# A state space layer between large matrix products: response matrices stored lag by lag and loaded a tile ahead, transposes one piece later, and the small products that prepare them four at one priority

## The chip, the core and the metric

The kernel runs on one core of one Trainium2 chip. The metric is the device time of that core in microseconds (us), from the start of the program to its end, in fp32 throughout. The kernel before took 2952.3, 2959.95 and 2960.65 us in three runs; the median is 2959.95.

## The reference, cut to what matters

A decoder trunk of two layers works on 256 positions of 2048 numbers. Each layer is a token mixer, an attention to 256 rows of memory (4 heads of 512) and an MLP with a hidden width of 8192 and a squared ReLU, each with an RMSNorm ahead of it and its result added to x. The mixer of layer 0 is a gated MLP. The mixer of layer 1 is a state space layer, and the change is there:

```python
lam_bar = jnp.exp(lam * dt)                      # 128 groups x 64 complex states
b_bar = ((lam_bar - 1.0) / lam)[..., None] * bmat
u = (h @ w_in).reshape(bsz, seq, 128, 16)        # 128 groups of 16 channels
bu = einsum('gpc,bsgc->sbgp', b_bar, u)
states = scan over s of (states = lam_bar * states + bu)
y = einsum('gcp,sbgp->bsgc', cmat, states).real + d_skip * u
val, gate = split(gelu(y) @ w_out + b_out, 2)
x = x + val * sigmoid(gate)
```

The scan is not run position by position. The 256 positions are cut into 32 chunks of T = 8. Inside a chunk the output is a product of the chunk's inputs with a matrix of responses to each lag (with d_skip at lag 0); the state that a chunk leaves behind is another product of its inputs; states are carried over chunks; and what the carried state adds to a chunk's outputs is a third product. The three matrices depend on the weights alone.

## The kernel before, in words

**The large products.** Nearly all of the time goes into products of the activations with weights. To keep fp32 accuracy on TensorE (PE), a weight tile of 128 x 1024 numbers (512 KB, `wraw`, four buffers) is loaded by SyncE's queue (line 118), rounded by ScalarE (ACT) into `whi` (L101), and what the rounding leaves is computed by VectorE (DVE) into `wlo` (L102); both have three buffers. The activations are split the same way. A product is then three matmuls: high by high, high by low, low by high (L145 to L147, in the MLP L558 to L560; with the roles exchanged two matmuls of 512 and 256 columns, L163 and L165). One weight tile with its 12 matmuls is called a *piece* here. Each function for large products calls `tick` after every piece (L148, L561).

**What sets the order.** The kernel is written in a framework that puts every operation into one list with priorities, by default in the order in which the program issues it. From this list it makes one queue for each engine and gives out the buffers; each engine then works strictly through its own queue. Work besides the large products comes in by `tick`: `at(delay, fn)` issues `fn` a number of pieces later (L76), and the list `side` gives out one function every `every` pieces (L81 to L88), at a lower priority: `later(100)` puts its operations some 100 places further back among the others, one by one, so that neighbours in the program can end up apart. Every load and store named below, other than of weights, goes by GpSimd's queue (POOL), which issues its DMAs in order, and a DMA into a buffer waits there until the buffer is free.

**The preparation** (`ssm_prep`) runs as side work under the MLP of layer 0. The 128 groups are taken in 32 quads of four, with three side functions for each. `quad` loads the quad's weights `bcq` (L769), turns the sign of half of them on DVE (L770) and computes `bb`. `quad_q` computes `qt`, 16 columns for each of nine powers (0 to 8), stores powers 1 to 8 as Qd (L796), and multiplies `bb` with `qt` in four small matmuls, one for each group, 32 rows of one PSUM bank each (L799). `kd`, 15 lags by 16 numbers on 128 partitions, gets zeros for the seven negative lags by POOL (L802), lags 1 to 7 by ACT, lag 0 with d_skip by DVE, and is stored as Kd (L806). `quad_p` computes the matrix for the states, transposes it on PE (L814) and stores it as Pd (L817). Eight groups, two quads, share one tile of Pd, Qd and Kd in memory (half `l` = q % 2), so there are 16 of each. In Kd the 15 lags of one input channel, half and group stand together: 15 x 16 numbers in a row.

**The state space stage** (`s5`) takes the product with `b_w_in` in four tiles of 512 columns, `n` = 0 to 3, of eight pieces each; a tile's small work runs under the pieces of the next ones. After the tile's product, DVE and ACT copy it to `u` (L853, L856). Then, by `follow`: two pieces later `inputs` transposes u (eight transposes, L867) and ACT copies it to `us` (L868); three pieces later `own` loads four tiles of `pq` from Pd and multiplies us with them (64 small matmuls, L881) into `z`; five pieces later `states` transposes z (L897) into `vv`; from six to nine `carry` runs the scan over chunks on DVE; after 13 and 15 `outputs` loads `dq` from Kd and `qq` from Qd, two of each at a time, and multiplies us with dq (L932) and vv with qq (L938); after 17 `features` applies the gelu (`y`) and transposes back (L950). Each load is written where its product is (`load`, L837 to L840), and the buffers bound how early it can run: four for pq, three for dq, two for qq. dq takes a window of eight lags for each position j in the chunk, in the address pattern `[[16, T], [8 * row, 16], [row, 8], [1, P]]`: 1024 runs of 128 numbers (512 bytes). pq and qq are read in rows of 4 KB. At the end of the stage come the products with `b_w_out`, whose results go by way of `val` and `gat` into x (L998 to L1010).

## Time and profile before

| | |
|---|---|
| three runs, median (us) | 2952.3 to 2960.65, 2959.95 |
| the profiled execution, its own time (us) | 2960.98 |
| its span, first to last instruction (us) | 2959.3 |
| mean clock granted to TensorE | 0.988 |
| PE busy | 2883.9 us, 97% of the span |
| DVE busy | 1834.4 us, 62% |
| ACT busy | 1337.5 us, 45% |
| POOL busy | 169.0 us, 6% |
| moved by DMA | 581.60 MB, mean 197 GB/s |

The profile is of one execution. A row of matmuls names line, tile, shape and how many stand together (x8); PEld is the loading of the stationary operand, which runs beside PE. A matmul in fp32 (the small ones here) is made in two passes and counts as two. A busy time is the sum of the durations, in which matmuls overlap, so that an engine at 100% can still be slower than at full clock; the granted clock (1.00 is full speed) tells that. A wait is put down to what ended it last. In rows of DMAs the time is that from issue to landing.

### The profile page before, as it was taken

What the parts mean: (1) busy time and instruction counts of PE and PEld (TensorE: products, weight loads), DVE (VectorE), ACT (ScalarE), POOL (GpSimd) and SP (SyncE); (2) the same over time, 40 slices, a digit from 0 to 9 for tenths busy, and PEclk for the clock granted to TensorE, in tenths of its full rate; (3) what the DMA queues carried; (4) which work ended last, traced back from release to release, by engine and by line L of the source; (5) the groups of instructions that cost most, each with busy time, mean ns of one, the idle gap of its engine ahead of it and who ended that gap; (6) DMA issues with size and microseconds to landing.
All of it is one profiled execution on the core that took longest, in us unless ns stands there. A gap on an engine that the chain in (4) does not pass through costs nothing.

```text
span 2959.3 us, 39341 instructions
## 1 busy us (share of the span) xinstructions
PE 2883.9 (97%) x15238; PEld 2379.4 (80%) x15238; DVE 1834.4 (62%) x2548; ACT 1337.5 (45%) x1714; POOL 169.0 (6%) x288
## 2 busy tenths in 40 slices
PE   8999999999999999999997899999999999999998
PEld 6878888888878778778875678888888888888886
DVE  5665655585768778677565455755556555465555
ACT  6435544445434434344453344544454434344443
POOL 1000000000011111111012100000000000000000
PEclk9999999999999999999998999999999999999999
DMA  8766666568666667666689957665566666666665
GB/s 278 213 180 191 193 178 179 170 179 239 190 201 213 206 208 218 205 206 203 215 221 236 206 177 211 192 178 180 169 187 189 187 188 188 186 191 187 188 186 150
DMA packets 180460, 581.60 MB, mean 197 GB/s; under 512 B 38592, under 2 KB 38896, under 8 KB 179504
## 3 DMA queue, kind: packets, MB, share of 16 engines
q1 hardware_dynamic: 140864, 509.67, 57.0%
q0 software_dynamic: 39264, 69.35, 9.2%
q8 instruction: 119, 1.95, 0.3%
q14 instruction: 69, 0.57, 0.1%
q10 hardware_dynamic: 144, 0.07, 0.0%
HBM read 553.88 MB, written 24.90 MB: 196 GB/s over the span
## 4 chain that ended last, share of the span: by engine, by line
PE 88%; DMA 6%; issue 3%; DVE 2%; ACT 1%; POOL 0%; SPq 0%; DVEq 0%; ACTq 0%; POOLq 0%
PE acc L163 23%; PE acc L165 12%; PE acc L560 8%; PE acc L558 8%; PE acc L559 8%; PE acc L146 8%; PE acc L147 7%; PE acc L145 7%; DMA dq<-Kd 1%; DMA qq<-Qd 1%; PE ps L799 1%; PE ps L494 1%; PE ps L438 1%; DMA wraw<-in_b_w_in 1%; DVE wlo L102 1%
## 5 line engine op out<-in xcount | busy, mean ns | idle before, releaser
L102 DVE TENSOR_TENSOR wlo<-wraw,whi 128x1024 fp32r<-128x1024 f32 x952 | 1164.4, 1224 | 891.1 <-ACT whi L101 888.7
L101 ACT CAST whi<-wraw 128x1024 fp32r<-128x1024 f32 x952 | 1002.1, 1053 | 1322.2 <-PE acc L163 409.3
L163 PE MATMUL acc<-act,whi 128*128 128x512 f32 x3072 | 1084.1, 396 | 0.6 <-ACT whi L101 0.6
L165 PE MATMUL acc<-act,wlo 128*128 128x256 f32 x3072 | 864.8, 282 | 0.9 <-DVE wlo L102 0.8
L163 PEld LDWEIGHTS acc<-act,whi 128*128 128x128 f32 x3072 | 576.0, 188 | 136.5 <-issue 4.6
L165 PEld LDWEIGHTS acc<-act,wlo 128*128 128x128 f32 x3072 | 580.2, 189 | 6.3 <-issue 3.0
L146 PE MATMUL acc<-wlo,act 128*128 128x512 f32 x1248 | 494.8, 396 | 13.8 <-DVE wlo L102 13.6
L145 PE MATMUL acc<-whi,act 128*128 128x512 f32 x1248 | 496.1, 397 | 9.6 <-ACT whi L101 9.6
L147 PE MATMUL acc<-whi,act 128*128 128x512 f32 x1248 | 492.6, 395 | 0.0
L560 PE MATMUL acc<-whi,hl 128*128 128x512 f32 x992 | 396.4, 400 | 0.0
L558 PE MATMUL acc<-whi,hh 128*128 128x512 f32 x992 | 396.0, 399 | 0.0
L559 PE MATMUL acc<-wlo,hh 128*128 128x512 f32 x992 | 395.0, 398 | 0.0
L146 PEld LDWEIGHTS acc<-wlo,act 128*128 128x128 f32 x1248 | 238.0, 191 | 69.0 <-DVE wlo L102 21.2
L145 PEld LDWEIGHTS acc<-whi,act 128*128 128x128 f32 x1248 | 238.1, 191 | 62.7 <-ACT whi L101 12.3
L147 PEld LDWEIGHTS acc<-whi,act 128*128 128x128 f32 x1248 | 237.9, 191 | 48.9 <-DVE act L102 0.4
L560 PEld LDWEIGHTS acc<-whi,hl 128*128 128x128 f32 x992 | 186.3, 188 | 48.6 <-issue 4.4
L559 PEld LDWEIGHTS acc<-wlo,hh 128*128 128x128 f32 x992 | 186.3, 188 | 48.4 <-issue 3.6
L558 PEld LDWEIGHTS acc<-whi,hh 128*128 128x128 f32 x992 | 186.3, 188 | 46.8 <-issue 3.2
L542 DVE SCALAR_TENSOR_TENSOR x<-acc,r,x 128x512 f32<-128x512 f32 x62 | 43.6, 745 | 11.7 <-PE acc L560 11.7
L176 ACT ACTIVATE junk<-x 128x512 f32<-128x512 f32 x56 | 35.4, 632 | 24.4 <-DVE x L535 13.9
L938 PE MATMUL ps<-qq,vv 64*32 64x128 f32 x512 | 14.9, 350 | 32.3 <-DMA qq<-Qd 32.3
L524 DVE SCALAR_TENSOR_TENSOR r<-r 128x512 f32<-128x512 f32 x64 | 44.2, 690 | 1.4
(288 smaller groups left out, 1721.3 us busy)
## 6 DMA issues: line engine op xcount, KB each, us to landing
wraw<-in_f_w_up SPq DMA_DIRECT2D x256, 512.0 KB, 3.7
wraw<-in_f_w_down SPq DMA_DIRECT2D x256, 512.0 KB, 3.7
wraw<-in_a_w_in SPq DMA_DIRECT2D x64, 512.0 KB, 4.6
wraw<-in_x_w_q SPq DMA_DIRECT2D x64, 512.0 KB, 3.7
wraw<-in_x_w_k SPq DMA_DIRECT2D x64, 512.0 KB, 3.7
wraw<-in_x_w_v SPq DMA_DIRECT2D x64, 512.0 KB, 3.7
wraw<-in_x_w_o SPq DMA_DIRECT2D x64, 512.0 KB, 3.7
wraw<-in_b_w_out SPq DMA_DIRECT2D x64, 512.0 KB, 4.5
```

The costliest lines, as they stand in the source:

```text
L101: self.nc.scalar.copy(out=hi, in_=src)
L102: self.nc.vector.tensor_tensor(out=lo, in0=src, in1=hi.bitcast(F32), op=ALU.subtract)
L145: nc.tensor.matmul(out[t], ah[:, kt, sl], hi[:, kk, :], start=st, stop=False)
L146: nc.tensor.matmul(out[t], ah[:, kt, sl], lo[:, kk, :], start=False, stop=False)
L147: nc.tensor.matmul(out[t], al[:, kt, sl], hi[:, kk, :], start=False, stop=en)
L163: nc.tensor.matmul(acc[:, f, :], hi[:, kk, sl], both[:, kt].rearrange("p a s -> p (a s)"), start=st, stop=False, skip_group_check=True)
L165: nc.tensor.matmul(acc[:, f, 0:S], lo[:, kk, sl], ah[:, kt, :], start=False, stop=en, skip_group_check=True)
L524: nc.vector.scalar_tensor_tensor(out=r, in0=r, scalar=0.0, in1=r, op0=ALU.max, op1=ALU.mult)
L542: nc.vector.scalar_tensor_tensor(out=xc, in0=acc[:, t, :], scalar=r2[:, t:t + 1], in1=xc, op0=ALU.mult, op1=ALU.add)
L558: nc.tensor.matmul(acc[:, t, :], ah[:, kt % 4, sl], hi[:, kk, :], start=st, stop=False)
L559: nc.tensor.matmul(acc[:, t, :], ah[:, kt % 4, sl], lo[:, kk, :], start=False, stop=False)
L560: nc.tensor.matmul(acc[:, t, :], al[:, kt % 4, sl], hi[:, kk, :], start=False, stop=en)
```

## The change

Four things are changed.

- The four products of a quad in `quad_q` get the same priority: the g-th is issued with its priority raised by g, the number of places that it stands behind the first.
- Kd has another layout: the lag comes ahead of half and group, so that for one input channel and one lag the 2 x 4 x 16 numbers of the tile stand together. A quad's `kd` is stored by four DMAs instead of one, one for each group, 16 partitions each with rows of 16 numbers. The window of eight lags that dq reads is then one row of 1024 numbers (4 KB) for each position and channel.
- The loads are taken out of `own` and `outputs`. `fetch` issues them: the four pq of tile 0 ahead of the loop, those of tile n + 1 four pieces after tile n's product, dq and qq of tile n six and eight pieces after it. dq, qq and pq have four buffers each. To make room, `y` takes the buffer of `z`, and `val` and `gat` take the buffers of pq.
- `inputs` and `own` come one piece later (3 and 4 instead of 2 and 3); `states`, `carry`, `outputs` and `features` stay.

```diff
         mk = lambda nm, sh: [self.dram.tile(sh, F32, name=f"{nm}{q}") for q in range(G // 8)]
         self.Pd = mk("Pd", [P, 2, 4, P])
         self.Qd = mk("Qd", [2, 64, 2, 4 * P])
-        self.Kd = mk("Kd", [32, 2, 4, NL, 16])
+        self.Kd = mk("Kd", [16, NL, 2, 4, 16])
         self.TC1 = self.const.tile([P, 3, G // 2], F32, name="TC1")
         self.TC2 = self.const.tile([P, 3, 2, G // 2], F32, name="TC2")
         sg = pool.tile([P, 1], F32, name="sg", bufs=1)
...
             nc.gpsimd.dma_start(out=self.Qd[q // 2][q % 2].rearrange("p r n -> r p n"), in_=qt[:, 1:])
             kp = self.ps([P, T, 16])
             for g in range(4):
-                nc.tensor.matmul(kp[32 * g:32 * g + 32], bb[:, g], qt[:, 0:T, g, :], start=True, stop=True,
-                                 skip_group_check=True)
+                with self.tc.high_priority(offset=g):
+                    nc.tensor.matmul(kp[32 * g:32 * g + 32], bb[:, g], qt[:, 0:T, g, :], start=True, stop=True,
+                                     skip_group_check=True)
             kd = pool.tile([P, NL, 16], F32, name="kd", bufs=2)
             nc.gpsimd.memset(kd[:, 0:T - 1, :], 0.0)
             nc.scalar.copy(out=kd[:, T:, :], in_=kp[:, 1:, :])
             v.scalar_tensor_tensor(out=kd[:, T - 1, :], in0=eye, scalar=dsk[:, q:q + 1], in1=kp[:, 0, :],
                                    op0=ALU.mult, op1=ALU.add)
-            nc.gpsimd.dma_start(out=self.Kd[q // 2][:, q % 2].rearrange("k t l c -> t k (l c)"), in_=kd)
+            for t in range(4):
+                nc.gpsimd.dma_start(out=self.Kd[q // 2][:, :, q % 2, t], in_=kd[32 * t:32 * t + 16])
         def quad_p(q):
             bcq, bb, tq = e.pop(q)
...
             yT = self.new_act()
             st = {}
-            def load(src, nm):
-                t = sp.tile([P, 2, 4, P], F32, name=nm, bufs={"pq": 4, "dq": 3, "qq": 2}[nm])
+            ahead = {}
+            def load(src, nm, shape):
+                t = sp.tile(shape, F32, name=nm, bufs={"pq": 4, "dq": 4, "qq": 4}[nm])
                 nc.gpsimd.dma_start(out=t, in_=src)
                 return t
+            def fetch(nm, n, i):
+                if nm == "pq":
+                    t = load(self.Pd[4 * n + i], nm, [P, 2, 4, P])
+                elif nm == "qq":
+                    t = load(self.Qd[4 * n + i].rearrange("l p r n -> (l p) r n"), nm, [P, 2, 4 * P])
+                else:
+                    kd = self.Kd[4 * n + i]
+                    t = load(bass.AP(tensor=kd.tensor, offset=kd.offset,
+                                     ap=[[P, T], [(2 * T - 1) * P, 16], [1, T * P]]), nm, [P, T * P])
+                ahead[nm, n, i] = t
             def chunks(n, acc):
...
                 for h in range(2):
                     pz = self.ps([P, 2, 2, 2, 64])
                     for i in range(2):
-                        pq = load(self.Pd[4 * n + 2 * h + i], "pq")
+                        pq = ahead.pop(("pq", n, 2 * h + i))
                         for l in range(2):
                             for t in range(4):
                                 nc.tensor.matmul(pz[32 * t:32 * t + 32, i, l].rearrange("p r s -> p (r s)"),
...
                 if half == 0:
                     st[n] += [[self.ps([P, 4, P]) for _ in range(2)]]
                 py = st[n][2]
-                row = (2 * T - 1) * 16
                 for i in (2 * half, 2 * half + 1):
-                    kd = self.Kd[4 * n + i]
-                    dq = load(bass.AP(tensor=kd.tensor, offset=kd.offset,
-                                      ap=[[16, T], [8 * row, 16], [row, 8], [1, P]]), "dq")
-                    qq = load(self.Qd[4 * n + i].rearrange("l p r n -> (l p) r n"), "qq")
-                    qv = qq.rearrange("p r a b -> p r (a b)").rearrange("p r (j t c) -> p r t j c", t=4, c=16)
+                    dq = ahead.pop(("dq", n, i)).rearrange("p (j l t c) -> p l t j c", j=T, l=2, t=4)
+                    qq = ahead.pop(("qq", n, i))
+                    qv = qq.rearrange("p r (j t c) -> p r t j c", t=4, c=16)
                     for l in range(2):
                         for t in range(4):
-                            nc.tensor.matmul(py[l][32 * t:32 * t + 32, i, :], us[:, 2 * i + l, t, :], dq[:, l, t, :],
+                            nc.tensor.matmul(py[l][32 * t:32 * t + 32, i, :], us[:, 2 * i + l, t, :], dq[:, l, t],
                                              start=(i == 0), stop=False, skip_group_check=True)
                     for r in range(2):
                         for l in range(2):
...
             def features(n):
                 py = st.pop(n)[2]
-                y = sp.tile([P, T, 4, 2, 16], F32, name="y", bufs=1)
+                y = sp.tile([P, T, 4, 2, 16], F32, name="y", tag="z", bufs=1)
                 for l in range(2):
                     nc.scalar.activation(out=y[:, :, :, l, :].rearrange("p j i c -> p i j c"),
                                          in_=py[l].rearrange("p i (j c) -> p i j c", j=T), func=AF.Gelu)
...
             def follow(n):
-                self.at(2, lambda: inputs(n))
-                self.at(3, lambda: own(n))
+                for i in range(4):
+                    if n + 1 < NCH:
+                        self.at(4, lambda i=i: fetch("pq", n + 1, i))
+                    self.at(6 + i // 2 * 2, lambda i=i: fetch("dq", n, i))
+                    self.at(6 + i // 2 * 2, lambda i=i: fetch("qq", n, i))
+                self.at(3, lambda: inputs(n))
+                self.at(4, lambda: own(n))
                 self.at(5, lambda: states(n))
                 self.at(6, lambda: [carry(n, 2, 15), carry(n, 4, 7, 2)])
                 self.at(7, lambda: [carry(n, c, 1, 4) for c in (8, 12, 16)])
...
                 self.at(15, lambda: outputs(n, 1))
                 self.at(17, lambda: features(n))
+            for i in range(4):
+                fetch("pq", 0, i)
             for n in range(NCH):
                 acc = self.gemm_tok(hT, a["b_w_in"], n)
                 if n == 0:
...
                 cs = slice(j * NB, (j + 1) * NB)
                 bv = self.bc(sp, a["b_b_out"][j * NB:(j + 1) * NB])
                 bg = self.bc(sp, a["b_b_out"][D + j * NB:D + (j + 1) * NB])
-                val = sp.tile([P, 2, NB], F32, name="val", bufs=1)
-                gat = sp.tile([P, 2, NB], F32, name="gat", bufs=1)
+                val = sp.tile([P, 2, NB], F32, name="val", tag="pq", bufs=4)
+                gat = sp.tile([P, 2, NB], F32, name="gat", tag="pq", bufs=4)
                 b2 = lambda b: b.unsqueeze(1).broadcast_to([P, 2, NB])
                 if j == 1:
                     for t in range(2):
```

The order of TensorE's queue in the preparation, at the first quad: whi and wlo belong to the MLP's product, `bb` and `qt` to the quad. First the order of before.

```order
L559 MATMUL acc<-wlo,hh 128x512
L799 MATMUL ps<-qt,bb 32x128
L560 MATMUL acc<-whi,hl 128x512
L799 MATMUL ps<-qt,bb 32x128
L558 MATMUL acc<-whi,hh 128x512
L799 MATMUL ps<-qt,bb 32x128
L559 MATMUL acc<-wlo,hh 128x512
L799 MATMUL ps<-qt,bb 32x128
```

Each of the four stands alone there. The same place with the change:

```order
L559 MATMUL acc<-wlo,hh 128x512
L801 MATMUL ps<-qt,bb 32x128 x4
L560 MATMUL acc<-whi,hl 128x512
L558 MATMUL acc<-whi,hh 128x512
L559 MATMUL acc<-wlo,hh 128x512
```

The four products now stand together. Over the whole preparation the 128 products stand in 95 stretches before (81 of one, 2 of two, 5 of three, 7 of four) and in 32 of four now.

POOL's queue in the preparation, from one load of bcq to the next, first before; the numbers behind Qd, Kd and Pd count the tiles in memory.

```order
L769 DMA bcq<-in_b_bc 128x256
L796 DMA Qd_5542<-qt 2x64x512
L806 DMA Kd_5558<-kd 4x32x240
L802 MEMSET kd 128x112
L817 DMA Pd_5526<-po 128x512
```

That is one store for each of the three matrices. The same quad with the change:

```order
L770 DMA bcq<-in_b_bc 128x256
L797 DMA Qd_5542<-qt 2x64x512
L809 DMA Kd_5558<-kd 240x1x16 x4
L820 DMA Pd_5526<-po 128x512
L804 MEMSET kd 128x112
```

One store of Kd became four, and the memset of a later kd stands ahead of the Pd store in some quads and behind it in others.

POOL's queue in the state space stage, from the loads of the last tile's pq (Pd_5536 to 5539) on: Kd_5560 to 5563 and Qd_5544 to 5547 belong to the second tile (n = 1), Kd_5564 to 5567 and Qd_5548 to 5551 to the third.

```order
L839 DMA pq<-Pd_5536 128x1024
...
L839 DMA dq<-Kd_5563 128x8x128
L839 DMA qq<-Qd_5546 128x1024
L839 DMA qq<-Qd_5547 128x1024
L839 DMA dq<-Kd_5564 128x8x128
L839 DMA dq<-Kd_5565 128x8x128
L839 DMA qq<-Qd_5548 128x1024
L892 MEMSET vv 128x2x16
```

The loads of two tiles stand mixed there. With the change, from the same four loads on:

```order
L844 DMA pq<-Pd_5536 128x1024
...
L844 DMA dq<-Kd_5564 128x1x1024
L844 DMA qq<-Qd_5548 128x1024
L844 DMA dq<-Kd_5565 128x1x1024
L844 DMA qq<-Qd_5549 128x1024
L844 DMA dq<-Kd_5566 128x1x1024
L844 DMA qq<-Qd_5550 128x1024
```

Before, loads of the second tile (Kd_5563, Qd_5546 and 5547) still stood behind the last tile's pq; now they stand ahead of it, and dq and qq of the third tile follow it directly, two by two. On TensorE's queue the first transposes of u stand behind as many gemm matmuls as before, counted from the stage's start 135 in the first tile (96 of the first tile's own product and 39 of the next), 82, 25 and 25 in the turns after it; the products with pq stand behind one matmul more in the first two turns and nine more in the last two. The loads of dq and qq of the first tile stand where TensorE has reached the last pieces of the MLP ahead of the stage.

## Prediction

> **What bounds the kernel now.** I read the page's 40 slices first, then the busy time by stretch, then TensorE's waits in the one stretch that stands out, and last the timeline inside it. The first block has PE's row of the slices (tenths of 74 us each). The second has two stretches: us, then busy time and count for PE, PEld, DVE, ACT and POOL, granted clock, DMA share, GB/s.
>
> ```profile
> PE   8999999999999999999997899999999999999998
> ```
> ```profile
> 780.00:1410.00 630.00, 630.00 (x3197) 497.94 (x3197) 476.61 (x749) 263.69 (x321) 93.49 (x160) 1.00 0.69 208
> 1480.00:1720.00 240.00, 199.02 (x1743) 153.77 (x1742) 129.98 (x272) 102.62 (x180) 38.04 (x48) 0.90 0.87 211
> ```
>
> TensorE (PE) is the bound nearly everywhere. While the prep runs under the first layer's MLP (780 to 1410 us) it is busy for all of 630 us; there, time is won only by giving it less to do. In the state space stage (1480 to 1720 us) it stands idle for 240 - 199.0 = 41.0 us, its clock falls to 0.90, and the DMA engines are 0.87 busy. Its waits in that stage (total us, times, longest):
>
> ```profile
> PE ps L938 <- DMA qq<-Qd: 32.3, 8, 9.0
> PE ps L867 <- ACT u L856: 5.0, 4, 2.4
> ```
>
> Most of it is waiting for matrices that are loaded just before use. A wait costs more than its length. The timeline (start, us, what, idle before) around the longest:
>
> ```profile
> 1575.10 1.11 PE L938 MATMUL ps<-qq,vv 64*32 64x128 f32 x32 [8.97 <-DMA qq<-Qd]
> ...
> 1580.19 0.63 PE L146 MATMUL acc<-wlo,act 128*128 128x512 f32 x1
> 1580.61 0.63 PE L147 MATMUL acc<-whi,act 128*128 128x512 f32 x1
> ```
>
> After 9 us without work the matmuls start 0.42 us apart; at full clock, below, it is 0.228.
>
> **Part 1: prep's products in fours.** Two pieces of PE's timeline: the four products of a quad with gemm matmuls between them (each product is two passes, so x2), and a quad whose four happen to stand together already (x8).
>
> ```profile
> 810.51 0.39 PE L558 MATMUL acc<-whi,hh 128*128 128x512 f32 x1
> 810.74 0.40 PE L559 MATMUL acc<-wlo,hh 128*128 128x512 f32 x1
> 811.07 0.41 PE L799 MATMUL ps<-qt,bb 128*32 128x128 f32 x2
> 811.40 0.50 PE L560 MATMUL acc<-whi,hl 128*128 128x512 f32 x1
> 811.84 0.41 PE L799 MATMUL ps<-qt,bb 128*32 128x128 f32 x2
> ```
> ```profile
> 922.77 0.28 PE L165 MATMUL acc<-act,wlo 128*128 128x256 f32 x1
> 922.88 0.39 PE L163 MATMUL acc<-act,whi 128*128 128x512 f32 x1
> 923.11 0.28 PE L165 MATMUL acc<-act,wlo 128*128 128x256 f32 x1
> 923.32 0.43 PE L799 MATMUL ps<-qt,bb 128*32 128x128 f32 x8
> 923.68 0.50 PE L163 MATMUL acc<-act,whi 128*128 128x512 f32 x1
> 924.02 0.28 PE L165 MATMUL acc<-act,wlo 128*128 128x256 f32 x1
> ```
>
> One product alone: 811.84 - 811.07 = 0.77 us from one to the next, less the gemm matmul between them (0.23, from 810.51 to 810.74) leaves 0.53. Four together: a pair of L165 and L163 takes 0.34 (922.77 to 923.11); from 923.11 to 924.02 are 0.91 us with one pair, so 0.91 - 0.34 = 0.57. A stretch of products costs about 0.53 to 0.57 whether it has one or four. In the order of before the 128 products stand in 95 stretches, in that of the change in 32. That takes away 63 x 0.53 = 33.4 us, all on PE in a stretch where PE never waits.
>
> What could give it back is the feeder. VectorE has 476.6 us of work in 630, which would be 80% of the shorter 597, and PE shows no wait there; I count nothing. The same quads now send their lag products out in four stores instead of one, each on POOL's queue: three more issues, in runs of 64 bytes (one lag of 16 numbers) instead of 960. Behind them in POOL's queue stand the memset of a later kd, which waits for the stores, the Pd store and the load of the next bcq, and for bcq waits DVE's sign flip (L770), a few instructions on in the queue that also splits the weights. The rows: POOL's wait ahead of the bcq load, the Kd store's issue (min, median, max), and three DMAs with KB each and median us to landing.
>
> ```profile
> POOL bcq L769 <- DVE tq L789: 80.8, 23, 7.6
> ```
> ```profile
> L806 POOL DMA_DIRECT2D Kd<-kd x32: 700/722/734, 814.9 to 1395.8; - x32
> ```
> ```profile
> pq<-Pd POOLq DMA_DIRECT2D x16, 512.0 KB, 7.6
> dq<-Kd POOLq DMA_DIRECT2D x16, 512.0 KB, 18.5
> ...
> Kd<-kd POOLq DMA_DIRECT2D x32, 120.0 KB, 5.5
> ```
>
> In 23 of 32 quads POOL reaches that load 80.8 / 23 = 3.5 us early. Three more issues take 3 x 0.72 = 2.2 of it. How long four stores of short runs take to land, no row shows. Bounds: below, four small stores (16 of 32 partitions each, so 15 KB, half the bytes in all) land sooner than the one of 120 KB (5.5), which gains nothing on PE; above, they grow like the load with the most runs: dq has 1024 runs and takes 18.5, pq has 128 and the same bytes and takes 7.6, a factor of 2.4, so 5.5 x 2.4 = 13.4. I take about the present landing, since in bytes and in POOL's cover they are nearest to that row, and 2 us in all for quads without cover.
>
> The Trainium skill, "DMA: Bandwidth & Descriptors", section "Specifications", speaks against this edit: transfers below 512 bytes miss line rate, because the DMA engine reads, modifies and writes. No run here shows such stores yet; by this rule the upper bound is the nearer one, and the sum is that of the second rival.
>
> **Part 2: the stage at full pace.** What would the stage's work take without waits? The counts come from the groups of the stage, the times from a piece where nothing waits.
>
> ```profile
> L938 PE MATMUL ps<-qq,vv 64*32 64x128 f32 x512 | 14.9, 350 | 32.3 <-DMA qq<-Qd 32.3
> L932 PE MATMUL ps<-dq,us 128*32 128x128 f32 x256 | 12.3, 315 | 0.4 <-ACT vv L901 0.3
> ...
> L881 PE MATMUL ps<-pq,us 128*32 128x128 f32 x256 | 9.3, 307 | 0.3
> ```
> ```profile
> 1595.98 1.95 PE L881 MATMUL ps<-pq,us 128*32 128x128 f32 x64
> ...
> 1598.43 0.40 PE L147 MATMUL acc<-whi,act 128*128 128x512 f32 x1
> ...
> 1602.53 0.39 PE L147 MATMUL acc<-whi,act 128*128 128x512 f32 x1
> 1602.76 1.04 PE L897 MATMUL ps<-ident,z 128*128 128x128 f32 x8
> 1603.73 0.64 PE L932 MATMUL ps<-dq,us 128*32 128x128 f32 x16
> 1604.30 0.69 PE L938 MATMUL ps<-qq,vv 64*32 64x128 f32 x32
> 1604.92 0.64 PE L932 MATMUL ps<-dq,us 128*32 128x128 f32 x16
> ```
>
> From 1598.43 to 1602.53 are 18 gemm matmuls: 0.228 each. Eight transposes take 0.97 (1602.76 to 1603.73), 16 of L932 0.57, 32 of L938 0.62, 64 of L881 1.95. Of the 1743 matmuls 1024 are of these three lines and 104 are transposes; 615 are gemm. Sum: 615 x 0.228 = 140.1, 4 x 1.95 = 7.8, 13 x 0.97 = 12.6, 16 x 0.57 = 9.1, 16 x 0.62 = 9.9: 179.5. The stage takes 240, so 60.5 us are over: 41.0 idle, 19.5 at the slow clock.
>
> What of it goes? The loads are made about a turn ahead. A turn (one tile of 512 columns) is 96 x 0.228 + 1.95 + 3 x 0.97 + 4 x (0.57 + 0.62) = 31.5 us. In the order of the change dq and qq of a tile are issued as the products of the tile before give up their buffers, some 29 us before use, and pq likewise; against landings of 18.5 and 7.6 (qq, in the same queue, lies between) the waits of 32.3 end, with the slow clock behind them. dq also lies in memory in runs of 4 KB now, like pq. The first tile's twelve loads are issued before and at the stage's start, in the last pieces of the MLP.
>
> What stays? The transposes one piece later: as the order has it, the first ones of each tile stand behind as many gemm matmuls as before (39 in the first turn, 25 in the third); only the pq products behind them move, by 1 matmul in two turns and 9 in the others. So I keep 4.3 of the 5.0 us of waiting for u (its copies are paced by the same weight splits), and take the longer room for the copy of us as worth nothing, up to 1 us. 2.2 stay for the change between small products and gemm matmuls (20 times 0.11: the L163 at 923.68 above is followed after 0.34 instead of 0.23), and 2 for the weight loads that share the first microseconds with four matrices. 60.5 - 8.5 = 52.0 go.
>
> The shared buffers (y with z, val and gat with pq) put no wait in: z of a tile is read out a piece after it is written and y comes pieces later, and pq is done long before val. Without that cover a wait would be one piece, 2.7 us, for a tile.
>
> **The sum.** The profiled execution took 2961.0 (span 2959.3 and 1.7 around it): 2961.0 - 33.4 + 2 - 52.0 = 2877.6. It stands 1.0 over the median of 2959.95, so 2877.
>
> **The rivals.** First, the loads are early and still late, since the DMA engines are the bound. A turn moves 12 matrices and 8 weight tiles of 0.524 MB, 10.5 MB. The fastest stretch of the stage:
>
> ```profile
> 1600.00:1605.00 5.00, 5.00 (x73) 3.90 (x76) 2.18 (x2) 3.09 (x5) 0.30 (x1) 1.00 1.01 404
> ```
>
> At 404 GB/s a turn's bytes take 26.0 us of 31.5, at the stage's present 211 they take 49.8. The first is against this rival, the second for it; dq's short runs are the likely reason of the 211, and they go. Half way, 37.9, three turns are late by 6.4 each: 2877 + 19 = 2896, with ends of 2887 and 2877 + 3 x 18.3 = 2932. A mechanism that would bring it: dq uses half of the DMA engines, which then carry 8.4 / 16 + 2.1 / 8 = 0.79 MB a turn each; at 404 / 16 = 25 GB/s that is 31.1 us, no room at all. That is how the skill's page on DMA ("Why a DMA increments its semaphore by 16 and not by 1", on how many engines) reads for a source whose outermost size is 8, with an exception for some copies from GpSimd. No run here shows which holds.
>
> Second, slower: the short stores hold up prep. The place is POOL's memset and the bcq load behind it; the price 13.4 - 5.5 + 2.2 - 3.5 = 6.6 us a quad, on DVE and so on PE, 32 times: 211, so 3088. It decides from the point where the net delay passes (33.4 + 52) / 32 = 2.7 us a quad. Against it: 18.5 was measured with qq in the same queue at a share of 0.87, prep has 0.69 and a quarter of the bytes.
>
> Third, PE's saving in prep comes to nothing because DVE takes over: 2877 + 33 = 2910. For it, 80% busy in bursts; against it, no wait of PE in 630 us.
>
> That the change does not do what it says is not left open: the order shows both moves.
>
> **How the numbers follow.** My forecast (2868 to 2887) has 0.62, the first rival 0.19, the third 0.07, the second at its price 0.07, a part of it that eats up the gain 0.02, anything else on the fast side 0.03. Under 0.3%, 9 us, a measurement of this kernel tells nothing from no change. So faster 0.91, same 0.02, slower 0.07. The range reaches from 2868 to 2918: forecast, third rival and most of the first, about 0.84.
>
> **What would show it.** Right: prep's products only as x8 in the timeline, and some 33 us less from the first quad's to the last's; no wait of PE for qq, dq or pq, and the stage's clock near 1.00. Wrong: a wait of PE for wlo in prep with DVE waiting for bcq (second rival), PE waits for dq or qq in the second half of a turn and weights landing over 10 us (first), or DVE near 100% in prep (third).

## The result, and the profile after

The change takes 2885.2 us (median of four runs, 2881.5 to 2887.5) where the kernel before takes 2956.7 beside it: a ratio of 0.9757, with a 95% interval of 0.9743 to 0.9772. That is 71.5 us less, about 2.4%; 2877 was forecast, with a range of 2868 to 2918. The profiled execution took 2886.2, with a span of 2884.4.

First the slices of PE after, then its busy times (columns as before): the stretch of the preparation, and the stage from its first gemm matmul to the first L163 behind it.

```profile
PE   8999999999999999999989999999999999999998
```
```profile
780.80:1374.00 593.20, 593.20 (x3177) 486.69 (x3177) 473.32 (x747) 260.70 (x320) 141.67 (x256) 1.00 0.72 217
1443.80:1770.00 326.20, 313.10 (x2305) 251.37 (x2304) 204.18 (x343) 162.46 (x253) 30.62 (x57) 0.98 0.82 236
```

The same stage before, as a row of its own:

```profile
1480.20:1845.50 365.30, 324.28 (x2306) 257.29 (x2305) 205.08 (x343) 162.95 (x253) 42.33 (x56) 0.93 0.82 211
```

The stage is 39 us shorter: 41.0 us of idle time have become 13.1, and the clock has risen from 0.93 to 0.98. What PE still waits for in it (us, times, longest):

```profile
PE ps L884 <- ACT u L873: 8.3, 3, 4.0
PE acc L146 <- DVE wlo L102: 2.3, 4, 0.8
PE acc L145 <- ACT act L101: 1.4, 1, 1.4
```

Four waits of 0.6 us and less are left out. The waits for qq (32.3) are gone, and none for dq or pq has come. The waits for u, 5.0 before, have grown. In the preparation the products stand together, as PE's timeline at the first quad shows:

```profile
807.79 0.40 PE L559 MATMUL acc<-wlo,hh 128*128 128x512 f32 x1
808.12 0.43 PE L801 MATMUL ps<-qt,bb 128*32 128x128 f32 x8
808.47 0.50 PE L560 MATMUL acc<-whi,hl 128*128 128x512 f32 x1
808.81 0.39 PE L558 MATMUL acc<-whi,hh 128*128 128x512 f32 x1
```

Since the order of the large products is the same in both kernels, the start of one and the same gemm matmul can be looked up in each timeline. That cuts each run in pieces (us). "Preparation" is from the MLP's product under which it begins (783.7 before) to the state space stage, "stage" the row above; "first part" is the stage's first 192 gemm matmuls; "behind" goes from the stage's end to one of the last gemm matmuls, 37 us before the end of the program.

| kernel | preparation | stage | first part | rest of it | behind |
|---|---|---|---|---|---|
| before | 696.4 | 365.3 | 57.7 | 307.6 | 1076.4 |
| the change | 663.1 | 326.2 | 58.3 | 267.9 | 1077.1 |
| fours alone | 663.7 | 364.7 | 58.9 | 305.8 | 1076.3 |
| Kd lag by lag alone | 696.4 | 349.1 | 54.6 | 294.5 | 1075.9 |
| loads ahead alone | 696.4 | 335.6 | 61.9 | 273.7 | 1076.4 |
| buffers alone | 696.4 | 335.8 | 60.6 | 275.2 | 1077.2 |
| early transposes | 663.1 | 325.6 | 58.0 | 267.6 | 1076.4 |
| small work later | 662.9 | 325.2 | 54.7 | 270.5 | 1076.4 |
| first loads held back | 663.0 | 325.5 | 48.8 | 276.7 | 1076.5 |
| dq by eight DMAs | 663.0 | 329.9 | 48.8 | 281.2 | 1076.6 |
| dq channel first | 665.1 | 329.8 | 54.0 | 275.8 | 1076.8 |
| stores doubled | 664.8 | 326.4 | 59.3 | 267.1 | 1077.1 |
| grouped, later | 663.1 | 329.6 | 52.7 | 276.9 | 1076.8 |
| grouped, near | 663.9 | 337.1 | 58.3 | 278.7 | 1076.8 |

So the two profiles differ by 33.3 us in the preparation, 39.1 in the stage, and 3 in the 780 us ahead of both, where nothing was changed: the profiled execution of before was the slowest of all there (783.7 us to the start of the preparation's MLP, 777.2 to 782.9 in the other runs). The gain in the stage lies wholly behind its first part, which takes 57.7 us before and 58.3 after.

### The profile page after: what moved, and what is told of

The parts are those of the page before. It is cut to its first block, busy times and chain, and to the rows that moved or that the text cites. A ratio compares the mean times of both kernels' runs of the same rounds, so it can differ in the third digit from the quotient of the medians.

```text
span 2884.4 us, 39580 instructions
## 1 busy us (share of the span) xinstructions
PE 2837.0 (98%) x15238; PEld 2365.6 (82%) x15238; DVE 1831.7 (64%) x2548; ACT 1332.5 (46%) x1714; POOL 205.4 (7%) x384
## 4 chain that ended last, share of the span: by engine, by line
PE 90%; DMA 4%; DVE 3%; issue 2%; ACT 1%; POOL 0%; SPq 0%; DVEq 0%; ACTq 0%; POOLq 0%
PE acc L163 24%; PE acc L165 12%; PE acc L560 8%; PE acc L559 8%; PE acc L558 8%; PE acc L146 8%; PE acc L147 8%; PE acc L145 8%; DVE wlo L102 1%; DMA wraw<-in_b_w_in 1%; PE ps L494 1%; PE ps L438 1%; PE ps L214 1%; DMA memc<-in_mem 1%; DMA wraw<-in_f_w_up 0%
## 5 line engine op out<-in xcount | busy, mean ns | idle before, releaser
L163 PE MATMUL acc<-act,whi 128*128 128x512 f32 x3072 | 1080.4, 395 | 0.6 <-ACT whi L101 0.6
L163 PEld LDWEIGHTS acc<-act,whi 128*128 128x128 f32 x3072 | 576.1, 188 | 130.6 <-issue 1.6
L146 PEld LDWEIGHTS acc<-wlo,act 128*128 128x128 f32 x1248 | 236.6, 190 | 63.9 <-DVE wlo L102 16.9
L809 POOL DMA_DIRECT2D Kd<-kd x128 | 72.4, 580 | 186.4 <-issue 174.2
L542 DVE SCALAR_TENSOR_TENSOR x<-acc,r,x 128x512 f32<-128x512 f32 x62 | 43.7, 746 | 10.6 <-PE acc L560 10.5
L101 ACT CAST hh<-r 128x512 fp32r<-128x512 f32 x64 | 39.4, 615 | 16.6 <-DVE r L524 16.3
```

The lines of the kernel that those rows point to most:

```text
L101: self.nc.scalar.copy(out=hi, in_=src)
L146: nc.tensor.matmul(out[t], ah[:, kt, sl], lo[:, kk, :], start=False, stop=False)
L163: nc.tensor.matmul(acc[:, f, :], hi[:, kk, sl], both[:, kt].rearrange("p a s -> p (a s)"), start=st, stop=False, skip_group_check=True)
L542: nc.vector.scalar_tensor_tensor(out=xc, in0=acc[:, t, :], scalar=r2[:, t:t + 1], in1=xc, op0=ALU.mult, op1=ALU.add)
L809: nc.gpsimd.dma_start(out=self.Kd[q // 2][:, :, q % 2, t], in_=kd[32 * t:32 * t + 16])
```

## The experiments

### The parts one by one

The first four each bring one part to the kernel before. **Fours alone** (`e1`):

```diff
-                nc.tensor.matmul(kp[32 * g:32 * g + 32], bb[:, g], qt[:, 0:T, g, :], start=True, stop=True,
+                with self.tc.high_priority(offset=g):
+                    nc.tensor.matmul(kp[32 * g:32 * g + 32], bb[:, g], qt[:, 0:T, g, :], start=True, stop=True,
...
```

> The kernel before with nothing but the equal priority of a quad's four products. Theory (a stretch of products costs about 0.53 us on TensorE however many stand in it, and 63 stretches go): 33 us less than before, about 2924, all of it between the first and the last quad, and the state space stage as before, with 32 us of waits for qq. Rival (the fours only move the stretches' cost to VectorE or to the stores behind them, and the gain seen in the change's preparation comes from the smaller stores of Kd): under 10 us less.

Measured: 2922.8, ratio 0.9901 (0.9877 to 0.9925). The preparation is 32.7 us shorter and the stage as before, with 31.0 us of waits for qq. The fours are worth what a stretch costs times the stretches that go, and the smaller stores have no part in it.

**Kd lag by lag alone** (`e2`): layout, four stores and dq in rows of 4 KB, with loads and buffers as before.

```diff
-        self.Kd = mk("Kd", [32, 2, 4, NL, 16])
+        self.Kd = mk("Kd", [16, NL, 2, 4, 16])
...
-            nc.gpsimd.dma_start(out=self.Kd[q // 2][:, q % 2].rearrange("k t l c -> t k (l c)"), in_=kd)
+            for t in range(4):
+                nc.gpsimd.dma_start(out=self.Kd[q // 2][:, :, q % 2, t], in_=kd[32 * t:32 * t + 16])
...
-                                      ap=[[16, T], [8 * row, 16], [row, 8], [1, P]]), "dq")
+                                      ap=[[P, T], [(2 * T - 1) * P, 16], [1, T * P]]), "dq")
...
```

> The kernel before with nothing but the lag-by-lag Kd, its four stores and dq read in rows of 4 KB; loads and buffers (4, 3, 2) as before. Theory A (the waits for qq come from loads that are issued only some microseconds before use, because two qq buffers are too few): 20 us or more of waits for qq stay, and the time is within 12 us of before. Rival B (the short runs of dq are what slows POOL's queue and with it qq): dq lands in 8 to 10 us instead of 18.5, the waits for qq fall under 10 us, and the time is 35 us or more under before.

Measured: 2940.6, ratio 0.9958 (0.9944 to 0.9971), 12.8 us less. Its waits and its loads:

```profile
PE ps L940 <- DMA qq<-Qd: 22.3, 8, 6.9
```
```profile
dq<-Kd POOLq DMA_DIRECT2D x16, 512.0 KB, 12.8
qq<-Qd POOLq DMA_DIRECT2D x16, 512.0 KB, 12.1
```

Two thirds of the waits stay, as theory A had it, and the 12.8 us are just over its 12; but dq lands in 12.8 instead of 18.5 us (rival B had 8 to 10), and the stage is 16 us shorter with that. And the preparation takes 696.4 us, to the tenth what it takes with the one store: the four short stores cost nothing there.

**Loads ahead alone** (`e3`) is the change with the old products, the old Kd, its one store and the old dq pattern. The edit, cut to the pattern, is shown against the change:

```diff
                 else:
+                    row = (2 * T - 1) * 16
                     kd = self.Kd[4 * n + i]
                     t = load(bass.AP(tensor=kd.tensor, offset=kd.offset,
-                                     ap=[[P, T], [(2 * T - 1) * P, 16], [1, T * P]]), nm, [P, T * P])
+                                     ap=[[16, T], [8 * row, 16], [row, 8], [1, P]]), nm, [P, 2, 4, P])
...
```

**Buffers alone** (`e4`) is the kernel before, with nothing moved:

```diff
-                t = sp.tile([P, 2, 4, P], F32, name=nm, bufs={"pq": 4, "dq": 3, "qq": 2}[nm])
+                t = sp.tile([P, 2, 4, P], F32, name=nm, bufs={"pq": 4, "dq": 4, "qq": 4}[nm])
...
-                y = sp.tile([P, T, 4, 2, 16], F32, name="y", bufs=1)
+                y = sp.tile([P, T, 4, 2, 16], F32, name="y", tag="z", bufs=1)
...
-                val = sp.tile([P, 2, NB], F32, name="val", bufs=1)
-                gat = sp.tile([P, 2, NB], F32, name="gat", bufs=1)
+                val = sp.tile([P, 2, NB], F32, name="val", tag="pq", bufs=4)
+                gat = sp.tile([P, 2, NB], F32, name="gat", tag="pq", bufs=4)
```

> The change without the equal priority and with the old Kd, its one store and dq read in 1024 runs of 512 bytes: loads ahead, four buffers each and transposes one piece later alone. Theory A: no wait for qq or dq is left, and the time is 36 to 42 us under before, about 2918. Rival B (short runs): dq and qq land in over 25 us and waits of 15 us or more stay, so that under half of the stage's gain is there.

> The kernel before with nothing but more buffers: four of dq and of qq, y in z's buffer, val and gat in pq's; the loads are written where they were, the transposes come where they came, and Kd is the old one. POOL's queue then has the loads in the same order as the change. Theory A (only the number of buffers holds a load back): the same time as the run with the loads ahead, within 5 us. Rival C (that the loads are written earlier is needed): 15 us or more slower than that run, with waits for qq left.

Measured: 2928.2 with the loads ahead, ratio 0.9914 (0.9894 to 0.9933), and 2931.3 with the buffers, 0.9925 (0.9907 to 0.9943). The stage takes 335.6 and 335.8 us: writing the loads a tile ahead adds nothing to having the buffers, since POOL's queue runs as far ahead as buffers are free in both. About 25 us came with the loads ahead instead of the expected 36 to 42, and 22 with the buffers. With the short runs the loads are slow, and late now and then (waits and loads of `e3`):

```profile
PE ps L883 <- ACT u L872: 9.7, 4, 5.1
PE ps L951 <- DMA qq<-Qd: 3.6, 2, 2.0
...
PE ps L945 <- DMA dq<-Kd: 1.1, 2, 0.6
```
```profile
dq<-Kd POOLq DMA_DIRECT2D x16, 512.0 KB, 20.8
qq<-Qd POOLq DMA_DIRECT2D x16, 512.0 KB, 22.9
```

In the stage the buffers give 29.5 us and the layout 16.2, each alone, and 39.1 together, less than the sum: in part they take away the same waits.

### What is left in the stage

All that follow are built on the change. **Early transposes** (`e5`): `inputs` and `own` back at two and three pieces.

```diff
-                self.at(3, lambda: inputs(n))
-                self.at(4, lambda: own(n))
+                self.at(2, lambda: inputs(n))
+                self.at(3, lambda: own(n))
```

> The change with inputs and own two and three pieces after the tile, as before. In TensorE's queue only the products with pq move, by one gemm matmul in two turns and nine in two. Theory (this part of the change is worth nothing either way): within 4 us of the change, about 2885, with 7 to 9 us of waits for u. Rival (own one piece later spares TensorE a wait for us): 6 us or more slower than the change, with waits for us in place of none.

Measured: 2886.0, ratio 0.9770 (0.9756 to 0.9784), with 8.2 us of waits for u. This part of the change is worth nothing that can be measured.

**Small work later** (`e6`), the loads of pq and the scan likewise:

```diff
+                d = int(n < NCH - 1)
-                self.at(3, lambda: inputs(n))
-                self.at(4, lambda: own(n))
-                self.at(5, lambda: states(n))
+                self.at(3 + d, lambda: inputs(n))
+                self.at(4 + d, lambda: own(n))
+                self.at(5 + d, lambda: states(n))
...
```

> The change with inputs, own, the loads of pq, states and the scan another piece later for the first three tiles. The transposes of u move back by 2, 2, 11 and 1 gemm matmuls. Theory (TensorE stands at the transposes for 8.3 us because ACT's and VectorE's copies to u come between their weight splits; the slow clock after these waits costs about as much again): the wait goes where the distance is 11 (2.6 us and the clock behind it) and shrinks by 0.5 where it is 2: 3 to 6 us less than the change. Rival (the wait only moves on, to the products with pq or dq): within 2 us of the change or slower.

Measured: 2879.1, ratio 0.9749 (0.9734 to 0.9764): the lowest median of all, with an interval that overlaps the change's. The waits for u fall by 4.0, and others come:

```profile
PE ps L884 <- ACT u L873: 4.3, 3, 2.3
PE ps L952 <- DMA qq<-Qd: 2.5, 1, 2.5
PE ps L898 <- ACT us L885: 1.4, 1, 1.4
PE acc L147 <- DVE act L102: 1.4, 1, 1.4
```

The stage gains 3.6 us in its first part and loses 2.6 in the rest. By the profile the rival is right: the wait moves on. But the profiled execution took 2884.6 us and the other three 2876.6 to 2879.9, so it does not settle whether the theory's 3 to 6 us are there.

**First loads held back** (`e9`): each buffer of the first tile's dq and qq gets one column of u ahead of its load, so that the load waits for u.

```diff
+                if first:
+                    nc.gpsimd.tensor_copy(out=t[:, 0:1] if len(shape) == 2 else t[:, 0, 0:1],
+                                          in_=st["u0"][:, 7, 7, 15:16])
...
```

> The change with the first tile's dq and qq held back on POOL until u of the first tile is written (a copy of one column of u into each buffer ahead of its load). Theory (these eight matrices, 4.2 MB issued as the stage begins, make the stage's first weights late, the late weights hold up ACT's casts, and the copies to u stand between the casts): weights of the stage's first 35 us wait less, the first wait for u falls from 4.0 us to 2 or less, the waits for wlo before it (2.3 us) go: 4 to 7 us less than the change. Rival (the copies of u are late by the order on ACT and VectorE alone): the first wait stays at 3 us or more and the time within 2 us of the change.

Measured: 2883.1, ratio 0.9756 (0.9742 to 0.9770), no different from the change. Its stage in stretches:

```profile
1443.00:1476.00 33.00, 33.00 (x151) 27.34 (x150) 22.48 (x41) 19.77 (x35) 5.15 (x15) 1.00 0.65 186
1476.00:1508.00 32.00, 26.90 (x178) 21.12 (x177) 20.91 (x52) 17.75 (x36) 2.65 (x5) 1.00 1.03 274
1508.00:1540.00 32.00, 29.97 (x353) 23.21 (x354) 22.24 (x55) 14.24 (x24) 6.87 (x13) 0.89 0.93 271
```

With the eight matrices issued some 23 us later the first part takes 48.8 us instead of 58.3, 9.5 less, with no wait worth naming. In ACT's timeline the casts up to the last copy to u stand idle for 17.8 us in all until their weights land in the change, 16.9 in the kernel before, and not at all in this run: the late weights were the cause of the first waits, as the theory says, and in the kernel before as well. But the loads now meet the second tile's pq, PE waits 4.1 for u and 1.8 for pq there, the clock falls to 0.89, and the rest takes 8.8 us more. The time did not come: the same bytes crowd the next turn.

**dq by eight DMAs** (`e7`):

```diff
...
+                    for j in range(T):
+                        nc.gpsimd.dma_start(out=t[16 * j:16 * j + 16],
+                                            in_=bass.AP(tensor=kd.tensor, offset=kd.offset + j * P,
+                                                        ap=[[(2 * T - 1) * P, 16], [1, T * P]]))
...
```

> The change with dq loaded by eight DMAs of 16 rows of 4 KB, one for each position of the chunk, instead of one DMA of 8 x 16 rows. Theory (a load whose outermost size is 8 is carried by half of the DMA engines, so dq takes about twice the 7.6 us of pq): each part of dq lands in under 10 us, the other loads of the stage land sooner too, and with TensorE no longer waiting for matrices the time falls by at most 3 us. Rival (all engines are used anyhow and dq, qq and the weights share one rate): from the first issue to the last landing a dq takes 14 us or more, and POOL's 8 x 0.6 us for each dq puts qq 4 us or more behind: same or slower.

Measured: 2892.1, ratio 0.9794 (0.9775 to 0.9813), slower. Each part of dq lands in 5.9 us, qq in 6.3, and the first part takes 48.8 us. But POOL is busy for 82.4 us of the stage, and in the rest PE stands for 7.0 us at one place behind ACT's copies to u. Since POOL also spread the loads out in time, this run does not tell why they landed sooner.

**dq channel first** (`e10`) takes that out: one DMA, the same bytes and rows, with the partitions of dq in the order channel, position. u and prep's matrix must be written in that order too.

```diff
-                                     ap=[[P, T], [(2 * T - 1) * P, 16], [1, T * P]]), nm, [P, T * P])
+                                     ap=[[(2 * T - 1) * P, 16], [P, T], [1, T * P]]), nm, [P, T * P])
-                u = sp.tile([P, 8, T, 16], F32, name="u", bufs=1)
+                uc = sp.tile([P, 8, 16, T], F32, name="u", bufs=1)
+                u = uc.rearrange("p g c j -> p g j c")
...
```

> The change with the order of dq's partitions turned round, channel ahead of position, so that the outermost size of its load is 16 instead of 8; bytes, rows of 4 KB and the number of DMAs stay. u and prep's matrix for the states are written in the same order. Theory (with an outermost size of 8 half of the DMA engines carry dq): dq lands like pq, in under 10 us instead of 15.8, qq behind it in under 13 instead of 19.2, the stage's weights in under 7 instead of 8.0, and the stage is 6 to 12 us shorter, as the first turns of the run with eight DMAs were: about 2875. Rival (the eight DMAs helped only because POOL issued them slowly): dq lands in 14 us or more and the time is within 3 us of the change.

Measured: 2896.1, ratio 0.9793 (0.9779 to 0.9806), slower. The loads of the stage in the change, and then in this run:

```profile
wraw<-in_b_w_in SPq DMA_DIRECT2D x28, 512.0 KB, 8.0
dq<-Kd POOLq DMA_DIRECT2D x16, 512.0 KB, 15.8
qq<-Qd POOLq DMA_DIRECT2D x16, 512.0 KB, 19.2
pq<-Pd POOLq DMA_DIRECT2D x12, 512.0 KB, 7.1
```
```profile
wraw<-in_b_w_in SPq DMA_DIRECT2D x29, 512.0 KB, 5.1
dq<-Kd POOLq DMA_DIRECT2D x16, 512.0 KB, 10.6
qq<-Qd POOLq DMA_DIRECT2D x16, 512.0 KB, 12.9
pq<-Pd POOLq DMA_DIRECT2D x12, 512.0 KB, 5.4
```

Everything lands a quarter to over a third sooner; dq was expected under 10 us. In the loads of the stage only the order of dq's dimensions is different, with an outermost size of 16 instead of 8. The Trainium skill, "DMA: Bandwidth & Descriptors", section "Why a DMA increments its semaphore by 16 and not by 1", would say that this doubles the DMA engines; these landings agree, though no trace here counts engines. But the preparation takes 2.0 us more than with the change and the stage 3.6. For the stage the copies to u show why (ACT, then DVE; mean ns of one behind the busy time; first the change, then this run):

```profile
L873 ACT ACTIVATE u<-acc,rstd 32x128 f32<-32x128 f32 x64 | 19.5, 350 | 8.2 <-DVE u L870 7.7
L870 DVE TENSOR_TENSOR u<-acc,rstd 32x256 f32<-32x256 f32 x32 | 13.4, 418 | 1.0 <-ACT u L873 0.4
```
```profile
L874 ACT ACTIVATE u<-acc,rstd 32x128 f32<-32x128 f32 x64 | 23.8, 474 | 12.3 <-DVE u L871 12.0
L871 DVE TENSOR_TENSOR u<-acc,rstd 32x256 f32<-32x256 f32 x32 | 20.5, 640 | 3.1 <-ACT u L874 2.6
```

Written in steps of eight numbers, the copies take 640 and 474 ns instead of 418 and 350, and PE waits 12.1 us for u instead of 8.3. So with loads that land soon PE waits for these copies, and more than before.

**Grouped copies**, with the small work later as in `e6` (`e11`), and near (`e12`, the change with `inputs` at four pieces like `own`). The copies had taken turns between the two engines; now DVE does its eight, then ACT its sixteen.

```diff
-                for j in range(4):
-                    rows = slice(32 * j, 32 * j + 32)
-                    for t in range(4):
+                for t in range(4):
+                    for j in range(4):
+                        rows = slice(32 * j, 32 * j + 32)
```

> The run with the small work one more piece later (inputs, own, states and the scan of the first three tiles), and the copies to u grouped: first VectorE's eight, then ScalarE's sixteen, where they took turns, two and four, each turn waiting for the other engine and with a weight split between the turns. TensorE's transposes stand at the same places as in that run in the first three tiles and two matmuls earlier in the last. Theory (what is left of the waits for u is this taking of turns: four turns of 0.83 and 1.23 us with a split of 1.05 or 1.23 in each, so that two hops instead of eight end 2 to 4 us sooner): the waits for u fall from 4.3 us to under 2, and the time is 3 to 6 us under that run's 2879. Rival (the weights that land late hold the copies up, however they are ordered): the waits for u stay at 4 us or more, and so does the time, within 3 us.

> The change with the copies to u grouped in the same way and inputs at four pieces like own, all else as in the change; the transposes stand 41 gemm matmuls behind the tile in every turn (39, 39, 30 and 29 in the change), the products with pq 3 behind them. Theory: the waits for u (8.3 us in the change) fall under 2; TensorE waits about 1 us a turn for us instead, 3 to 4 in all, since a copy of 1.1 us has only 3 x 0.23 in front of the products: 5 to 8 us under the change, about 2879. Rival (late weights): waits for u of 5 us or more and a time within 3 us of the change.

Measured: 2887.2 and 2896.1, ratios 0.9778 (0.9762 to 0.9794) and 0.9803 (0.9789 to 0.9817). The waits for u are gone in the first and 0.9 us in the second, as the theory says. Neither gains the time, and the second is slower than the change. What the first waits for instead:

```profile
PE acc L146 <- DVE wlo L102: 6.9, 6, 2.6
PE acc L145 <- ACT act L101: 5.0, 1, 5.0
PE ps L898 <- ACT us L885: 3.6, 1, 3.6
```

and ACT's timeline at the last and then at the second of these:

```profile
1547.52 1.04 ACT L101 CAST whi<-wraw 128x1024 fp32r<-128x1024 f32 x1 [5.37 <-DMA wraw<-in_b_w_in]
1548.47 1.07 ACT L885 COPY us<-ps 128x512 f32<-128x512 f32 x2
```
```profile
1572.62 4.96 ACT L873 ACTIVATE u<-acc,rstd 32x128 f32<-32x128 f32 x16 [1.92 <-DVE u L870]
1577.60 1.07 ACT L101 CAST act<-ps 128x512 fp32r<-128x512 f32 x2
```

At the wait of 3.6 us ACT stands for 5.4 us at a cast whose weights have not landed, with the copy that PE needs next behind it in the queue. The wait of 5.0 us has another cause, the grouping itself: the split of the activations (act), which PE needs next, stands behind all sixteen copies to u. In the change it stands behind eight of them, and the wait is 1.4. So the theory was right about u and wrong about the time: the taking of turns was what kept u, and with the copies grouped PE waits for the splits behind them and for late weights.

**Stores doubled** (`e8`): each quad's four stores a second time, to a tile that nobody reads.

```diff
...
             for t in range(4):
                 nc.gpsimd.dma_start(out=self.Kd[q // 2][:, :, q % 2, t], in_=kd[32 * t:32 * t + 16])
+            for t in range(4):
+                nc.gpsimd.dma_start(out=self.Kx[q // 2][:, :, q % 2, t], in_=kd[32 * t:32 * t + 16])
```

> The change with each quad's four stores of Kd issued twice, the second time to a tile of its own that nobody reads: eight stores in runs of 64 bytes for each quad. Theory (the short stores have room behind them in POOL's queue; the run with the stores alone lost nothing in the preparation): 4 x 0.58 = 2.3 us more of issue and a later landing for each quad, no wait on TensorE, within 4 us of the change. Rival (the preparation is near the point where POOL's memset and the load of bcq hold up VectorE): 30 us or more slower, with VectorE waiting for bcq over 2 us a quad.

Measured: 2889.9, ratio 0.9770 (0.9757 to 0.9784), an interval that overlaps the change's. The preparation takes 1.7 us more than with the change. DVE's waits for bcq:

```profile
DVE bcq L772 <- DMA bcq<-in_b_bc: 41.5, 22, 4.3
```

They grow from 24.6 to 41.5 us, 1.3 a quad, and PE waits 1.4 us in all.

## Why the prediction was right, and by how much it was off

- **The fours: right.** 63 stretches of 0.53 us, 33.4 in all, were forecast; the preparation is 33.3 us shorter, and 32.7 with this part alone. (The rows shown, 0.77 less 0.23, give 0.54 a stretch and 34.0 in all; nothing hangs on it.)
- **The stores: no price at all.** The 2 us for quads without cover were not there: 696.4 us with one store of 120 KB and with four of 15 KB. Landing was forecast at the present 5.5 us and is 5.6:

```profile
Kd<-kd POOLq DMA_DIRECT2D x128, 15.0 KB, 5.6
```

  Where "DMA: Bandwidth & Descriptors" ("Specifications") in the Trainium skill speaks against runs under 512 bytes, the trace agrees so far that an eighth of the bytes takes as long, though no run here tells how much of that is the short runs. Whatever the price is, PE does not wait for it. The second rival fell: even eight stores a quad do not reach it.
- **The stage: right in kind, off by 13 of 52 us.** The waits for qq and dq ended as forecast, 39.1 us came, and 21.4 of the 60.5 stayed instead of 8.5. Of them 13.1 are idle time, where 4.3 for u and 2 at the start were forecast, and 8.3 are work at less than full pace, where 2.2 were; three stretches of 32 us at a granted clock of 0.95, below, make some 5 of them.
- **The step that was mis-sized** is "2 for the weight loads that share the first microseconds with four matrices". Eight matrices meet them (dq and qq of the first tile, issued within 5 us), and the stage's first part loses 9.5 us to that: the run with the loads held back takes 48.8 where the change takes 58.3. The kernel before, with five matrices there, takes 57.7: this loss was among the 60.5 us already, and nothing in the change was to end it. Moving the loads does not end it either, since that run loses 8.8 us in the rest. "I keep 4.3 of the 5.0 us of waiting for u" hung on the same: the first wait for u grew from 2.4 to 4.0. That is 9.5 of the 21.4 us that stayed; the others lie in the rest of the stage, with its waits of 1.7 and 2.6 us for u and 1.4 for act and its slow clock.
- **The slow clock did not go "with" the waits for qq.** Some of it stayed, beside other waits: 0.95 in the stretch that holds the pause of 4.0 us for u, 1.00 in the next, whose longest pause is 1.7.

```profile
1476.00:1508.00 32.00, 27.26 (x177) 21.85 (x176) 19.32 (x44) 19.61 (x39) 2.10 (x4) 0.95 0.79 271
1508.00:1540.00 32.00, 30.31 (x370) 23.89 (x369) 27.67 (x69) 17.79 (x34) 6.86 (x13) 1.00 0.88 248
```

  The two stretches of 32 us behind these have 0.95 as well, with longest pauses of 2.6 and 1.4 us. So the length of a pause alone does not tell what the clock does.

- **The first rival** named the right resource and the wrong place: PE never waits for dq or qq, but the weights that share the DMA engines with them land in 8.0 us in the stage. Its reason, a load on half of the engines, fits the landings of the run with dq channel first. That run also shows that the loads alone do not hold the time.
- **The third rival** fell: DVE has 473.3 us of work in 593.2, the 80% that was forecast, and PE is busy throughout.
- **The sum.** 2961.0 - 33.3 - 39.1 is 2888.6; the 780 us ahead take 3.0 off, the part behind the stage adds 0.7, and 2886.2 was measured in the profiled execution. So of the 13 us that the stage fell short, the total shows under 9: 2 come from stores that cost nothing, and the 3 from a place that the change does not touch, which is luck.

**What stays open:** why the stage keeps some 20 us over its work. The first loads, the place of the small work and the copies' order were each changed, and each time the stage came out at 325 to 337 us with other waits. That fits weights and matrices that share a rate, and two engines whose queues hold both splits and copies, but no run removed both at once: the load of dq with 16 as its outermost size and u still written side by side was not tried.

## What to carry to other kernels

When a load is late, count its buffers before moving the line that issues it: an in-order DMA queue runs as far ahead as they allow, and here four buffers alone gave the stage all that writing the loads a tile ahead gave. Small matmuls between large ones cost by the stretch here (0.53 us) and not by the piece, so bring them together. When the last waits of a crowded stage move on each time one is removed, look for the shared rate and for queues in which urgent copies stand behind splits of late data, or urgent splits behind copies.

## What the hardware showed that was not expected

- Turning the outermost size of a 512 KB load from 8 to 16, with the same rows of 4 KB, brought its landing from 15.8 to 10.6 us, and that of the weights beside it from 8.0 to 5.1.
- Writes in steps of eight fp32 numbers instead of side by side: 640 instead of 418 ns for 32 x 256 on DVE, 474 instead of 350 for 32 x 128 on ACT; prep's products of 128 x 512 on DVE went from 689 to 1205 ns.
- The granted clock did not follow the longest pause of TensorE in a stretch of 32 us: 0.95 with pauses of 4.0, 2.6 and 1.4 us, 1.00 with one of 1.7.
